# Values of four query tiles in one burst, and W_out landing in the keys' ring, in a two-layer decoder trunk

## The chip, the cores and the metric

The kernel runs on one core of one Trainium2 chip. The metric is the device time of one execution in microseconds (us); each kernel is run several times and the median stands. A profile is one execution with the hardware profiler on. The engines are called as the profile does: PE is TensorE (matmuls; PEld its weight loads), DVE is VectorE, ACT is ScalarE, POOL is GpSimd, SP is SyncE, which here issues all DMAs from one queue in order.

## The reference

Two layers over a sequence of 1024 tokens of width 1024, each with a main branch and a memory branch, both gated, and a LayerNorm on the residual. Layer 0's main branch is a causal pooling. Layer 1's is an attention with a forget gate over 16 heads of 64, whose keys and values come from one projection of the stream:

```python
for block of 128 queries:
    logits = q @ k.T * 64 ** -0.5 + (cum[t] - cum[s])      # causal, cum: running sum of log forget gates
    p = softmax(where(mask, logits, -inf))
    out = p @ v
y = concat([out * silu(g_main), y_mem * silu(g_mem)])       # 1536 wide
x = layer_norm(4 ** 0.25 * x + y @ w_out[1])
```

## The kernel before

All float32 products are made of two or three matmuls of a high and a low part (`hi_lo`: ACT copies the high part in fp32r, DVE subtracts it from the source). A weight of 1 MB is a *slab*: it comes in two pieces of 256 KB, each is loaded to a buffer of the ring "raw" (four buffers), split into high and low in the ring "w" (six buffers, so three pieces), and used by 24 matmuls 128x512; a slab has 48 (L180), 24576 columns. While `low[0]` is set, which is the case in the attention of layer 1, POOL does the splits of slabs (L145, L146).

The change lies in the attention of layer 1, function `fox`. It runs over 16 heads, in pairs. A head has eight *steps*; step i makes tile 7 - i of 128 queries, from the widest (1024 keys) to the narrowest. `probs` makes the logits on PE (L168, two halves in the PSUM ring "L" of two banks), adds the forget row R and takes the minimum on DVE (L715), and the exponential on ACT (L723). In the next step `halves` writes them as a high and a low half in float16 (L744 on ACT, L745 on DVE), and `turn` transposes both with one DMA from SP (L754) into a buffer of ring "T" (six buffers). `LAG` is 5: five steps after a tile's logits PE multiplies it with the values (`values`; matmuls 128x128 in float16, called a *burst* here). Before, an even tile starts a burst for itself and the tile above it: tiles 7 and 6 in step 6 of their head, then 5 and 4, 3 and 2, 1 and 0 in steps 0, 2 and 4 of the next. They go to one PSUM buffer O (one bank, 256 columns used), and two instructions on 64 partitions evict them (L770 ACT, L771 DVE).

PE's order is written out by hand (`tc.manual_schedule(engines={PE})`): logits of the step, a part of the fill (`FRAC`: 0.4), the burst if there is one, the rest of the fill (0.6). The *fill* is matrix work that doesn't depend on the tiles: projections of keys, queries and values of the next pair (three slabs), and gates. Pairs 0, 1, 3, 5 and 6 have three slabs, pairs 2, 4 and 7 four; the fourth or, in pair 7, all four are gates (`gate_ahead`, `late_gate`). Every step gets the same share of fill (`SHARE`). After the last head there are five more steps without logits (`hd == HEADS`), filled by `lead`, which is the first third of layer 1's output projection. A scheduler of the framework sets the order on the other engines, from its own idea of the times; only instructions marked as pinned keep their program order.

`OutProj` brings W_out of layer 1 as 24 pieces of 128x512. `fetch` loads a piece to "raw", `split` makes its high and low part in buffers that the attention no longer needs: the n-th pair of pieces goes to the n-th entry of `wtags`. During pair 7 (heads 14 and 15) pieces 0 to 7 are fetched and split, and `early` brings a third of the branch's output y (columns of the memory branch) for the first 256 tokens, by two DMAs to "raw". In the same time `late_gate` reads the outputs of pairs 3, 5 and 6 back (R, ring of two buffers, shared with the forget rows), multiplies them with their gates on POOL (L790) and stores them again.

The ring "B" has ten buffers of 4 KB per partition; a pair's keys and queries take six of them.

Of the kernel before, what the change touches and what calls it, by code (L numbers as in the profile page):

```python
# [18 lines left out]
P = 128  # L19
# [19 lines left out]
SHARE = (1,1,1,1,1,1,1,1)  # L39
# [32 lines left out]
def trunk_kernel(ctx, tc, x, xT, memT, win, wk, wv0, wv, wmk, wmv, wout, poolw, pscale, lng, lnb, bforget, out):  # L72
# [264 lines left out]
    class OutProj:  # L337
# [45 lines left out]
        def early(self, yh, yl):  # L383
# [153 lines left out]
    with tc.tile_pool(name="in1", bufs=1) as in1:  # L537

        def xy(shape=(P, S)):
            return sb(list(shape), "B", 10, F32R, in1)  # L540

# [208 lines left out]
        def turn(hd, i, two):  # L750

            n = 2 * i + 2
            pt[hd, i] = T([P, 2 * ST, P], F16)
            nc.sync.dma_start_transpose(pt[hd, i][:, :n, :], two[:, : n * P])  # L754

        def values(hd, c, o):

            (v, un), b = pairs[hd // 2][2], hd % 2
            acc = ps([P, 2 * P], "O", 1)
            for i in (2 * c, 2 * c + 1):  # L760
                mm3(
                    acc[:, (i % 2) * P : (i % 2) * P + P],
                    [
                        (v[:, b, 2 * j : 2 * j + 2, :].rearrange("p e d -> p (e d)"), pt[hd, i][:, e * (i + 1) + j, :])
                        for j in range(i + 1) for e in range(2)
                    ],
                )
            own, other = slice(64 * b, 64 * b + 64), slice(64 - 64 * b, P - 64 * b)
            oc = o[own, c * 2 * P : (c + 1) * 2 * P]
# [6 lines left out]
        def pair_out(pr, c, o, g):  # L776

            for k in {1: (3, 2, 1), 0: (0,)}.get(c, ()) if g is not None else ():
                cols = slice(k * 2 * P, (k + 1) * 2 * P)
                nc.gpsimd.tensor_tensor(o[:, cols], o[:, cols], g[:, cols], ALU.mult)  # L780
            if c == 0:
                nc.sync.dma_start(y1d[pr // 4, :, pr % 4, :], o)
# [10 lines left out]
        def fox(following, out_proj):  # L793
# [8 lines left out]
            for hd in range(HEADS + 1):  # L802
# [15 lines left out]
                for i in range(ST if hd < HEADS else LAG):  # L818
                    tile_of = ST - 1 - i
                    ahead = sum(SHARE[i:]) + (sum(SHARE) if b == 0 else 0)  # L820
                    part = fill.left * SHARE[i] / (ahead if hd < HEADS else sum(SHARE[i:LAG]))
# [35 lines left out]
                    if older and older[1] % 2 == 0:  # L857
                        values(older[0], older[1] // 2, older[2])
                        if older[0] % 2:
                            pair_out(older[0] // 2, older[1] // 2, older[2], gs.get(older[0] // 2))  # L860
# [5 lines left out]
        wtags = [("MK", 4), ("V", 4)] + [("B", 10)] * 4 + [("w", 0), ("MK", 4), ("R", 2), ("V", 4), ("PG", 0), ("B", 10)]  # L866
# [69 lines left out]
```

## Time and profile before

| what | value |
|---|---|
| median of 3 runs | 1277.64 us (1276.83 to 1278.07) |
| profiled execution | 1276.2 us, its span 1274.5 us |
| granted clock of PE, mean | 0.992 |
| attention of layer 1 | about 664 to 1146 us of the span |
| PE busy there | 465.4 of 482.0 us |
| DVE, ACT, POOL busy there | 364.1, 324.3, 167.3 us |
| mean busy share of the 16 DMA engines there | 0.76 |

A row of a timeline has the start in us, the length of a merged group, the engine, the line of the kernel, the operation, what it writes and reads, and in brackets the idle time before it with what ended it. Rows of windows give busy time of PE, PEld, DVE, ACT and POOL with the count of instructions, then the granted clock, the share of the DMA engines and GB/s. Matmuls are pipelined: the time per matmul is read from one start to the next.

### The profile page before, as it was taken

To read this page: it belongs to the slowest core of one execution; us is meant where nothing else is said; L and a number is where in the kernel's file an instruction comes from. 1 tells how busy PE (TensorE), PEld (TensorE's weight loads), DVE (VectorE), ACT (ScalarE), POOL (GpSimd) and SP (SyncE) were. 2 spreads that over 40 slices of the span, in tenths; PEclk is the share of its full clock that TensorE was granted. 3 is DMA by queue.
4 is the path that set the end of the run, shared out by engine and by line. 5 is a ranking of instruction groups with operands and counts; after the bars stand their busy time and mean duration, and the time that the engine had idled before them with its cause. 6 is when DMAs were issued, how large, how long until landed. Compare 5 with 4: busy or idle time off the path is not lost. (4 is left out here: it accounts for less than half of the span.)

```text
span 1274.5 us, 19683 instructions
## 1 busy us (share of the span) xinstructions
PE 1245.2 (98%) x7018; PEld 1035.8 (81%) x7018; DVE 803.1 (63%) x1901; ACT 578.3 (45%) x1273; POOL 172.5 (14%) x276
## 2 busy tenths in 40 slices
PE   9999999999999999999999999999999998989997
PEld 6888888888888888888887778887888786868885
DVE  6444766366455555376457888777878887654644
ACT  5233643242321123266226677766767776542110
POOL 0000000000000000000013334343333332420000
PEclk9999999999999999999999999999999999989998
DMA  6333543242453323254517686867968697784430
GB/s 228 103 100 100 124 120 121 83 124 86 158 200 106 103 82 126 75 125 107 161 51 189 134 194 154 187 164 181 185 156 179 158 197 169 159 232 172 166 115 34
DMA packets 267427, 178.66 MB, mean 140 GB/s; under 512 B 212288, under 2 KB 225728, under 8 KB 267328
## 3 DMA queue, kind: packets, MB, share of 16 engines
q1 hardware_dynamic: 267328, 177.40, 52.6%
q8 instruction: 55, 0.90, 0.3%
q14 instruction: 44, 0.36, 0.1%
HBM read 94.97 MB, written 22.61 MB: 92 GB/s over the span
## 5 line engine op out<-in xcount | busy, mean ns | idle before, releaser
L180 PE MATMUL pj<-A,w 128*128 128x512 f32 x2928 | 725.3, 395 | 10.8 <-POOL w L145 9.2
L180 PEld LDWEIGHTS pj<-A,w 128*128 128x128 f32 x2928 | 537.2, 189 | 114.9 <-POOL w L145 9.6
L142 DVE TENSOR_TENSOR w<-raw,w 128x512 fp32r<-128x512 f32 x106 | 73.6, 695 | 105.5 <-ACT w L141 104.6
L723 ACT ACTIVATE T<-MK,s 128x512 f32<-128x512 f32 x192 | 110.8, 577 | 51.6 <-DVE s L715 39.2
L141 ACT CAST w<-raw 128x512 fp32r<-128x512 f32 x106 | 65.7, 621 | 149.0 <-PE pj L180 102.8
L745 DVE SCALAR_TENSOR_TENSOR P<-T,s,P 128x512 f16<-128x512 f32 x192 | 111.8, 614 | 31.6 <-ACT P L744 29.7
L744 ACT ACTIVATE P<-T,s 128x512 f16<-128x512 f32 x192 | 102.7, 576 | 46.4 <-ACT T L723 17.6
L168 PE MATMUL L<-B,B 128*128 128x512 f32 (+3 forms) x384 | 91.3, 343 | 5.0 <-DVE s L715 4.7
L168 PEld LDWEIGHTS L<-B,B 128*128 128x128 f32 x384 | 70.3, 188 | 25.9 <-DVE s L715 12.7
L620 POOL MEMSET G<- 128x128 f32 x1 | 0.2, 204 | 609.5 <-DVE V L334 609.5
L168 PEld LDWEIGHTS <-V 128*128 128x128 f16 x1152 | 66.8, 100 | 19.4 <-issue 18.9
L715 DVE CUSTOM_DVE_ANT_0 MK<-L,R 128x512 f32<-128x512 f32 (+3 forms) x128 | 72.9, 570 | 11.7 <-PE L L168 8.2
L168 PE MATMUL O<-T,V 128*128 128x128 f16 x1152 | 77.7, 223 | 1.7 <-DVE G L771 1.7
L142 DVE TENSOR_TENSOR T<-T,T 128x1024 fp32r<-128x1024 f32 x23 | 28.1, 1222 | 68.2 <-PE L L377 50.4
L146 POOL TENSOR_TENSOR w<-raw,w 128x512 fp32r<-128x512 f32 x54 | 69.7, 1291 | 3.8
L141 ACT CAST T<-T 128x1024 fp32r<-128x1024 f32 x23 | 24.2, 1052 | 99.0 <-DMA T<-y0d 50.5
L707 POOL TENSOR_SCALAR_AFFINE_SELECT R<-R 128x128 f32<-128x128 f32 x128 | 41.1, 327 | 172.3 <-DVE s L715 150.0
L145 POOL TENSOR_SCALAR w<-raw 128x512 fp32r<-128x512 f32 x54 | 35.4, 656 | 143.4 <-PE pj L180 130.4
L213 PE MATMUL pj<-T,w 128*128 128x256 f32 x384 | 48.7, 284 | 0.9 <-DVE w L142 0.8
L213 PEld LDWEIGHTS pj<-T,w 128*128 128x128 f32 x384 | 47.6, 192 | 2.0 <-DVE w L142 1.3
L377 PE MATMUL pj<-B,T 128*128 128x512 f32 x186 | 46.5, 392 | 0.5 <-DVE T L142 0.5
L377 PE MATMUL L<-B,T 128*128 128x512 f32 x174 | 43.0, 391 | 0.0
(214 smaller groups left out, 1598.6 us busy)
## 6 DMA issues: line engine op xcount, KB each, us to landing
raw<-in_win_dram SPq DMA_DIRECT2D x96, 256.0 KB, 2.8
raw<-in_wout_dram SPq DMA_DIRECT2D x48, 256.0 KB, 2.9
B<-B SPq DMA_DIRECT2D x32, 256.0 KB, 3.9
R<-cumd SPq DMA_DIRECT2D x16, 512.0 KB, 4.4
y0d<-Y SPq DMA_DIRECT2D x12, 512.0 KB, 3.1
T<-y0d SPq DMA_DIRECT2D x12, 512.0 KB, 4.1
T<-y1d SPq DMA_DIRECT2D x11, 512.0 KB, 4.0
raw<-in_wmk_dram SPq DMA_DIRECT2D x16, 256.0 KB, 2.6
```

The lines of the kernel that those rows point to most:

```text
L141: pin(nc.scalar.copy(hi, src))
L142: pin(nc.vector.tensor_tensor(lo, src, hi.bitcast(F32), ALU.subtract))
L146: nc.gpsimd.tensor_tensor(lo, src, hi.bitcast(F32), ALU.subtract)
L168: nc.tensor.matmul(acc, a, b, start=i == 0, stop=i == len(terms) - 1)
L180: nc.tensor.matmul(accs[n], a[:, k, :], b[:, kt, n * NH : (n + 1) * NH], start=kt == 0 and i == 0, stop=kt == KT - 1 and i == 2,)
L213: nc.tensor.matmul(acc, w[:, k, :], m[pc][:, k, :], start=pc == 0 and k == 0 and i == 0, stop=pc == 1 and k == 3 and i == 2,)
L377: nc.tensor.matmul(accs[a][nh], y[:, k, a * P : (a + 1) * P], w, start=kt == 8 and i == 0, stop=kt == 7 and i == 2,)
L707: nc.gpsimd.affine_select(R[:, qs], R[:, qs], [[-1, P]], ALU.is_ge, -NEG, base=0, channel_multiplier=1).ins
L715: nc.vector.tensor_tensor_reduce(p[:, lo:up], lg, R[:, lo:up], 1.0, top, ALU.add, ALU.min, m[:, n : n + 1])
L723: nc.scalar.activation(e, p[:, lo:up], AF.Exp, bias=top, scale=-1.0, accum_out=sums[:, n, hd % 2, i : i + 1],)
L744: nc.scalar.activation(pair[:, lo:up], e, AF.Copy, scale=r)
L745: nc.vector.scalar_tensor_tensor(pair[:, L + lo : L + up], e, r, pair[:, lo:up], ALU.mult, ALU.subtract)
```

## The change

- `values` takes four tiles at once: 7 to 4 (52 matmuls) in step 0 of the next head, and 3 to 0 (20 matmuls) in its step 4. O uses its whole bank of 512 columns, and the two evictions take 64x512 each. `pair_out` multiplies with the gate in two parts of two POOL instructions instead of three and one.
- Tiles 2 and 0 are transposed into the second half of the buffer of tiles 3 and 1, so a head takes six buffers of T instead of eight.
- The fill of a step is a share of what is left of fill and values together, less the step's own values: `VALUES` says that step 0 has 52 x 128 columns and step 4 has 20 x 128. It is never below zero.
- In pair 7 the first eight pieces of W_out are loaded by twos into buffers of ring B (`fetch_two`), in steps 0, 1, 5 and 11, and `early` loads its third of y by one DMA into a buffer of B, too. Their splits are placed anew, and the first three entries of `wtags` change places. Pieces 8 to 11 go to "raw" ahead of the five last steps.

```diff
-SHARE = (1,1,1,1,1,1,1,1)
+VALUES = {0: 52 * P, 4: 20 * P}
...
+        def fetch_two(self, land):
+
+            n = self.n + len(self.raws)
+            for j in range(2):
+                nc.sync.dma_start(land[:, j, :], wout[self.l, n // 2 % 2, 2 * self.KKS[n // 4] + j])
+                self.raws.append(land[:, j, :])
...
-            for j in range(2):
-                r, two = raw([P, 2, 2 * P]), slice(2 * j, 2 * j + 2)
-                nc.sync.dma_start(r, self.yd[2, :, two, : 2 * P])
-                yield
-                hi_lo(yh[:, two, :], yl[:, two, :], r, True)
+            nc.sync.dma_start(y, self.yd[2, :, :, : 2 * P])
+            yield
+            for two in (slice(0, 2), slice(2, 4)):
+                hi_lo(yh[:, two, :], yl[:, two, :], y[:, two, :], True)
                 yield
...
+        def land(shape):
+            return sb(list(shape), "B", 10, F32, in1)
...
-            pt[hd, i] = T([P, 2 * ST, P], F16)
-            nc.sync.dma_start_transpose(pt[hd, i][:, :n, :], two[:, : n * P])
+            if i in (2, 0):
+                to = pt[hd, i + 1][:, n + 2 :, :]
+            else:
+                to = T([P, 2 * ST, P], F16)
+            pt[hd, i] = to
+            nc.sync.dma_start_transpose(to[:, :n, :], two[:, : n * P])
...
-            acc = ps([P, 2 * P], "O", 1)
-            for i in (2 * c, 2 * c + 1):
+            acc = ps([P, NH], "O", 1)
+            for i in range(4 * c, 4 * c + 4):
...
-            oc = o[own, c * 2 * P : (c + 1) * 2 * P]
+            oc = o[own, c * NH : (c + 1) * NH]
...
-            for k in {1: (3, 2, 1), 0: (0,)}.get(c, ()) if g is not None else ():
+            for k in (2 * c + 1, 2 * c) if g is not None else ():
...
-                    ahead = sum(SHARE[i:]) + (sum(SHARE) if b == 0 else 0)
-                    part = fill.left * SHARE[i] / (ahead if hd < HEADS else sum(SHARE[i:LAG]))
+                    last = ST + LAG if hd == HEADS else (hd | 1) * ST + ST
+                    at = ST if hd == HEADS else hd * ST
+                    todo = [VALUES.get(k % ST, 0) if k >= ST else 0 for k in range(at + i, last)]
+                    part = max(0, (fill.left + sum(todo)) / len(todo) - todo[0])
...
-                        out_proj.fetch((0, 0, 1, 2, 3, 4, 5, 6, 6, 6, 7, 7, 7, 8, 8, 8)[step])
+                        if step in (0, 1, 5, 11):
+                            out_proj.fetch_two(land((P, 2, NH)))
                         if step == 9:
-                            lead = out_proj.early(*(xy((P, 4, 2 * P)) for _ in range(2)))
-                        if step in (9, 12):
+                            lead = out_proj.early(land((P, 4, 2 * P)), *(xy((P, 4, 2 * P)) for _ in range(2)))
                             next(lead)
+                    if hd == HEADS and i == 0:
+                        out_proj.fetch(12)
...
-                        out_proj.split((0, 0, 0, 1, 2, 3, 4, 5, 6, 6, 6, 6, 7, 7, 8, 8)[step], True)
-                        if step in (11, 15):
+                        out_proj.split((0, 0, 0, 1, 2, 3, 4, 5, 5, 5, 5, 6, 6, 6, 7, 8)[step], True)
+                        if step in (12, 13):
                             next(lead)
...
-                    if older and older[1] % 2 == 0:
-                        values(older[0], older[1] // 2, older[2])
+                    if older and older[1] % 4 == 0:
+                        values(older[0], older[1] // 4, older[2])
...
-        wtags = [("MK", 4), ("V", 4)] + [("B", 10)] * 4 + [("w", 0), ("MK", 4), ("R", 2), ("V", 4), ("PG", 0), ("B", 10)]
+        wtags = [("B", 10), ("V", 4), ("MK", 4)] + [("B", 10)] * 3 + [("w", 0), ("MK", 4), ("R", 2), ("V", 4), ("PG", 0), ("B", 10)]
```

Where the instructions stand is shown at three places. First SP's queue in head 14, before. The tiles named T with a transpose from P are the turned probabilities, raw the ring for loads; raw2303 is the second piece of W_in for late gate 3:

```order
L351 DMA raw2296_11920<-in_wout_dram 128x512
L754 DMA_TRANSPOSE T2284_11864<-P2275_11839 128x10x128
L782 DMA y1d_172<-G2040_10825 128x1024
L150 DMA raw2303_11941<-in_win_dram 128x512
L754 DMA_TRANSPOSE T2295_11911<-P2291_11897 128x8x128
L351 DMA raw2308_11996<-in_wout_dram 128x512
L754 DMA_TRANSPOSE T2306_11952<-P2301_11934 128x6x128
L150 DMA raw2330_12070<-in_win_dram 128x512
```

And now. Here raw2319 and raw2337 are the last two pieces of W_in of the pair (late gate 6); T2156 takes tile 0 of head 13, T2189, T2199 and T2213 take tiles 7, 6 and 5 of head 14:

```order
L150 DMA raw2319_12185<-in_win_dram 128x512
L570 DMA_TRANSPOSE V2161_11457<-MK2157_11445 128x16x64 x2
L767 DMA_TRANSPOSE T2156_11436<-P2171_11482 128x2x128
L767 DMA_TRANSPOSE T2189_11588<-P2186_11574 128x16x128
L150 DMA raw2337_12257<-in_win_dram 128x512
L767 DMA_TRANSPOSE T2199_11632<-P2196_11617 128x14x128
L767 DMA_TRANSPOSE T2213_11685<-P2208_11664 128x12x128
L358 DMA raw2347_12318<-in_wout_dram 128x512
```

The loads of W_in have moved ahead of head 14's transposes, and those of W_out that pass through raw are pieces 8 and later. Second, PE at the end of a burst in head 15's first step, before (O2334 the burst of tiles 5 and 4 of head 14, pj2328 a bank of the fill):

```order
L168 LDWEIGHTS V2215_11595
L168 MATMUL O2334_12083<-T2269_11814,V2215_11595 128x128
L180 MATMUL pj2328_12068<-A500_3025,w2332_12073 128x512
L180 MATMUL pj2328_12068<-A500_3025,w2331_12072 128x512
L180 MATMUL pj2328_12068<-A501_3026,w2331_12072 128x512
```

And now (O2272 the burst of tiles 7 to 4 of head 14, L2278 and L2280 the logits of tile 6 of head 15):

```order
L168 LDWEIGHTS V2161_11457
L168 MATMUL O2272_11927<-T2189_11588,V2161_11457 128x128
L168 MATMUL L2278_11991<-B2014_10810,B2061_11010 128x512
L168 MATMUL L2278_11991<-B2016_10812,B2061_11010 128x512
L168 MATMUL L2280_11998<-B2014_10810,B2061_11010 128x384
L168 MATMUL L2280_11998<-B2016_10812,B2061_11010 128x384
L180 MATMUL pj2267_11917<-A501_3026,w2270_11921 128x512
```

Fill followed the burst before; now the logits of the next tile do. Third, POOL around the first late gate, before (R2277 is the late gate's output, w and raw the splits of W_in, AFFINE_SELECT the mask on the forget row of head 15):

```order
L146 TENSOR_TENSOR w2305_11944<-raw2303_11941,w2304_11943 128x512
L145 TENSOR_SCALAR w2331_12072<-raw2330_12070 128x512
L146 TENSOR_TENSOR w2332_12073<-raw2330_12070,w2331_12072 128x512
L790 TENSOR_TENSOR R2277_11848<-R2277_11848,G2278_11849 128x256 x2
L145 TENSOR_SCALAR w2357_12187<-raw2356_12185 128x512
L790 TENSOR_TENSOR R2277_11848<-R2277_11848,G2278_11849 128x256 x2
L707 AFFINE_SELECT R2243_11710<-R2243_11710 128x128
L146 TENSOR_TENSOR w2358_12188<-raw2356_12185,w2357_12187 128x512
```

And now (R2222 the late gate's output, R2190 the forget row of head 15):

```order
L716 AFFINE_SELECT R2190_11599<-R2190_11599 128x128
L145 TENSOR_SCALAR w2320_12187<-raw2319_12185 128x512
L146 TENSOR_TENSOR w2321_12188<-raw2319_12185,w2320_12187 128x512
L803 TENSOR_TENSOR R2222_11748<-R2222_11748,G2223_11749 128x256 x4
L716 AFFINE_SELECT R2190_11599<-R2190_11599 128x128 x3
L145 TENSOR_SCALAR w2338_12259<-raw2337_12257 128x512
L146 TENSOR_TENSOR w2339_12260<-raw2337_12257,w2338_12259 128x512
L716 AFFINE_SELECT R2190_11599<-R2190_11599 128x128
```

The four multiplications of the late gate stand together now, ahead of three masks of head 15 and of the last split.

More of the change, by code (lines that the diff above doesn't have):

```diff
@@ L381, in products, with early @@
                             yield NH
-        def early(self, yh, yl):
-            for j in range(2):
-                r, two = raw([P, 2, 2 * P]), slice(2 * j, 2 * j + 2)
-                nc.sync.dma_start(r, self.yd[2, :, two, : 2 * P])
-                yield
-                hi_lo(yh[:, two, :], yl[:, two, :], r, True)
+        def early(self, y, yh, yl):
+            nc.sync.dma_start(y, self.yd[2, :, :, : 2 * P])
+            yield
+            for two in (slice(0, 2), slice(2, 4)):
+                hi_lo(yh[:, two, :], yl[:, two, :], y[:, two, :], True)
                 yield
@@ L752, in turn @@
             n = 2 * i + 2
-            pt[hd, i] = T([P, 2 * ST, P], F16)
-            nc.sync.dma_start_transpose(pt[hd, i][:, :n, :], two[:, : n * P])
+            if i in (2, 0):
[4 more added lines that the diff above has]
+            nc.sync.dma_start_transpose(to[:, :n, :], two[:, : n * P])
         def values(hd, c, o):
             (v, un), b = pairs[hd // 2][2], hd % 2
-            acc = ps([P, 2 * P], "O", 1)
-            for i in (2 * c, 2 * c + 1):
+            acc = ps([P, NH], "O", 1)
+            for i in range(4 * c, 4 * c + 4):
                 mm3(
-                    acc[:, (i % 2) * P : (i % 2) * P + P],
+                    acc[:, (i % 4) * P : (i % 4) * P + P],
                     [
@@ L856, in fox @@
                     older = past[0]
-                    if older and older[1] % 2 == 0:
-                        values(older[0], older[1] // 2, older[2])
+                    if older and older[1] % 4 == 0:
+                        values(older[0], older[1] // 4, older[2])
                         if older[0] % 2:
-                            pair_out(older[0] // 2, older[1] // 2, older[2], gs.get(older[0] // 2))
+                            pair_out(older[0] // 2, older[1] // 4, older[2], gs.get(older[0] // 2))
                     fill.pump(part * (1 - FRAC[0]))
```

## Prediction

> **What bounds the kernel now.** I read the page first: its first rows and the row of granted clock in section 2.
>
> ```profile
> span 1274.5 us, 19683 instructions
> PE 1245.2 (98%) x7018; PEld 1035.8 (81%) x7018; DVE 803.1 (63%) x1901; ACT 578.3 (45%) x1273; POOL 172.5 (14%) x276
> ...
> PEclk9999999999999999999999999999999999989998
> ```
>
> TensorE (PE) is the bound: 98% busy, and no other engine is near. So only three things can save time: PE's idle time, a slow clock, and pitch lost between matmuls. The clock row dips in slice 36 of 40 (1115 to 1147 us), and in the last, where the work ends. Then the waits of PE over the whole span:
>
> ```profile
> engine line waited for: us in total, times, longest us
> PE pj L180 <- POOL w L145: 9.2, 2, 5.5
> PE L L168 <- DVE s L715: 4.7, 11, 0.7
> PE O L168 <- DVE G L771: 1.7, 1, 1.7
> ```
>
> Two waits hold 9.2 us: a fill matmul (L180) that waits for GpSimd (POOL) to split a piece of W_in. The timeline of PE, and then of SP and POOL, around them:
>
> ```profile
> 1076.22 0.40 PE L168 MATMUL L<-B,B 128*128 128x256 f32 x2
> 1082.15 3.00 PE L180 MATMUL pj<-A,w 128*128 128x512 f32 x5 [5.54 <-POOL w L145]
> ...
> 1115.15 0.40 PE L168 MATMUL L<-B,B 128*128 128x256 f32 x2
> 1119.15 3.00 PE L180 MATMUL pj<-A,w 128*128 128x512 f32 x5 [3.61 <-POOL w L145]
> ```
>
> ```profile
> 1076.84 0.53 SPq L782 DMA_DIRECT2D y1d<-G  x1
> 1077.46 0.38 SPq L150 DMA_DIRECT2D raw<-in_win_dram  x1
> ...
> 1081.48 0.62 POOL L145 TENSOR_SCALAR w<-raw 128x512 fp32r<-128x512 f32 x1 [3.08 <-DMA raw<-in_win_dram]
> ...
> 1113.84 0.53 SPq L791 DMA_DIRECT2D y1d<-R  x1
> 1114.46 0.39 SPq L150 DMA_DIRECT2D raw<-in_win_dram  x1
> ...
> 1118.36 0.74 POOL L145 TENSOR_SCALAR w<-raw 128x512 fp32r<-128x512 f32 x1 [3.94 <-DMA raw<-in_win_dram]
> ```
>
> Both are the same event, in step 6 of head 14 and in step 6 of head 15 (the two matmuls 128x256 are tile 1). The piece of W_in was issued 4.0 us (1077.46 to 1081.48) and 3.9 us (1114.46 to 1118.36) before POOL could start on it, and PE ran dry meanwhile. The DMA was not slow; it was issued late. The order shows why: its buffer in the ring "raw" was held by W_out pieces, and it stood in SP's queue behind a store. What these stalls did to the clock, by windows:
>
> ```profile
> 1076.62:1082.15 5.53, 0.00 (x0) 0.00 (x0) 4.40 (x14) 3.74 (x9) 1.82 (x4) 0.82 1.05 262
> 1082.15:1087.00 4.85, 4.71 (x25) 3.39 (x25) 0.00 (x0) 0.00 (x0) 2.46 (x3) 0.50 0.74 190
> ...
> 1119.15:1124.60 5.45, 5.32 (x30) 3.98 (x31) 0.00 (x0) 0.00 (x0) 1.51 (x2) 0.50 0.98 209
> 1124.60:1130.00 5.40, 5.40 (x32) 4.53 (x30) 3.57 (x7) 3.77 (x9) 2.36 (x3) 1.00 0.64 170
> ...
> 1126.00:1146.60 20.60, 18.37 (x112) 14.66 (x111) 14.63 (x23) 12.10 (x23) 6.99 (x7) 1.00 0.75 229
> ```
>
> After each stall PE works for 4.85 and 5.45 us at a granted clock of 0.50, then at 1.00.
>
> **W_out in the keys' ring.** Pieces 0 to 7 of W_out no longer pass through "raw". In SP's new order the last two pieces of W_in for pair 7 stand ahead of the transposes of head 14's tiles 7 and 6, where before they stood in the middle of heads 14 and 15. They are needed ten steps later, so both stalls go: 9.15 us (5.54 + 3.61). The slow clock goes with them: half of 4.85 + 5.45 us, 5.15 us. What is late next? SP waits in turn for POOL to free a "raw" buffer, and so holds up a transpose by a step or so; POOL multiplies late gate 3 (four instructions, L803) before it masks R for tiles 6 to 4 of head 15. I put both into the new waits below. The pieces and their splits on ScalarE (ACT) and VectorE (DVE) stay the same in number; the early third of y comes in one DMA instead of two, and W_out in as many as before.
>
> [...]
>
> **One burst of four tiles.** The matmuls are the same ones, 1152 of values and all fills. What falls away is the change between the two kinds: 64 bursts become 32. Its price is read from a head with nothing in the way:
>
> ```profile
> 1021.96 1.85 PE L168 MATMUL O<-T,V 128*128 128x128 f16 x30
> 1023.61 1.41 PE L180 MATMUL pj<-A,w 128*128 128x512 f32 x5
> 1024.86 0.34 PE L168 MATMUL L<-B,B 128*128 128x128 f32 x2
> ...
> 1028.69 1.09 PE L180 MATMUL pj<-A,w 128*128 128x512 f32 x4
> 1029.62 1.40 PE L168 MATMUL O<-T,V 128*128 128x128 f16 x22
> 1030.83 1.41 PE L180 MATMUL pj<-A,w 128*128 128x512 f32 x5
> 1032.08 0.98 PE L168 MATMUL L<-B,B 128*128 128x512 f32 x4
> 1032.89 2.24 PE L180 MATMUL pj<-A,w 128*128 128x512 f32 x9
> 1034.97 0.85 PE L168 MATMUL L<-B,B 128*128 128x512 f32 x4
> ```
>
> From start to start, 30 values take 1.65 us and 22 take 1.21: 0.055 each and nothing left over. The nine fills without a burst take 2.08 us, 0.231 each; the five behind a burst take 1.25, against 1.155 at that rate. So a burst costs 0.095 us beyond its matmuls, and 32 fewer save 3.0 us. If a long burst cost twice as much the saving would be 0; if a boundary with the first fill was undercounted, 4. I keep 3.0.
>
> The evictions halve in number and double in width:
>
> ```profile
> L770 ACT ACTIVATE G<-O,unscale x64: 457/468/475, 693.8 to 1145.8; 64x256 f32<-64x256 f32 x64
> L771 DVE SCALAR_TENSOR_TENSOR G<-O,unscale,G x64: 457/484/492, 694.5 to 1146.6; 64x256 f32<-64x256 f32 x64
> ...
> L657 ACT ACTIVATE B<-pj x32: 581/592/595, 656.7 to 1041.0; 64x512 fp32r<-64x512 f32 x32
> ...
> L658 DVE SCALAR_TENSOR_TENSOR B<-pj,B x32: 683/688/695, 657.8 to 1042.1; 64x512 fp32r<-64x512 f32 x32
> ```
>
> Two 64x256 on DVE cost 0.97 us, one 64x512 (as L658) 0.69; ACT 0.94 against 0.59. Over 32 that frees 9.0 us of DVE and 11.0 of ACT. PE does not wait for that as such, so by itself I cost it at nothing: PE's 98% hides it. The bank is read out 1.28 us (0.59 + 0.69) after a burst, and the next burst is four steps away, so the wait of 1.7 us for it (at the end of head 15, where two bursts stood two steps apart) should go: 1.7.
>
> **Fills by steps.** Of each head, step 0 now holds 52 values and step 4 holds 20, and the fill is what levels the columns: in a pair with three slabs (73728 + 18432) / 16 = 5760 columns a step, less than 52 x 128 = 6656, so step 0 has no fill and the others about 11 matmuls instead of 9. The 4.7 us of waits of L168 for DVE fell on steps without a burst, where PE had 9 x 0.231 = 2.1 us between two logits; now it has 2.5. I take 2.9 of the 4.7 as gone (0 and 4.7 are the bounds).
>
> **The new waits.** A burst now starts directly behind the logits of tile 7, and needs tile 4's transpose. In the tightest head the transpose stood so (SP), with the landings of all 128 of them:
>
> ```profile
> 1024.60 1.79 SPq L754 DMA_TRANSPOSE T<-P  x1
> ...
> DMA to landing us min/median/max: 2.3/3.7/7.6
> ```
>
> Issued at 1024.60, used at 1029.62: 5.0 us. The 0.93 us of fill ahead of that burst (1028.69 to 1029.62) is gone, and 4.1 us stay, against a median of 3.7 and a maximum of 7.6. Nine of the sixteen bursts of tiles 7 to 4 fall in such short steps (in pairs with three slabs). Zero is one end; the other is 1 us in each of nine, 9. Most heads will fit as the median does; I take 2.5 for these, for POOL's new order and for SP's waits.
>
> **The sum.** - 9.15 - 5.15 - 3.0 - 1.7 - 2.9 + 2.5 = -19.4. The profiled execution took 1276.2 us (its span 1274.5), which becomes 1256.8. The median of the runs, 1277.64, is 1.4 above the profiled one, so I expect 1258.2, and say 1258.
>
> **Rivals.**
> (a) Transposes late. The bursts wait for tile 4 in the nine heads: 9 instead of 2.5, 1265. For it: a 0.4 us margin at the median. Against: not one burst of before waited for a transpose.
> (b) The stalls stay, or pair 7 gets a new one: SP in its order, blocked by POOL, holds the weights after all, and only the other terms come: 1277.6 - 3.0 - 1.7 - 2.9 + 2.5 = 1272.5. For it: L803 x4 stands ahead of masks and of the last split. Against: that split is needed only six steps on.
> [...]
> (d) More gain: all three waits go (4.7 + 1.7 + 9.15), with 5.15 of slow clock and 4 for the changes of kind, and nothing new comes: 1277.6 - 24.7 = 1253.
>
> **Chances.** My forecast with (d) as its lower end 0.78, (a) 0.10, (b) 0.06, (c) 0.04, a mixture near no change 0.02. The range runs from 1252 (just below (d)) to 1267 (past (a)) and leaves (b), (c) and some misses out. A difference of 0.2% (2.6 us) is about what a measurement can tell from none: faster 0.92, same 0.03, slower 0.05.
>
> **What would show it.** After: no row "PE pj L180 <- POOL w L145" of more than 1 us; clock 1.00 throughout heads 14 and 15; 32 groups of L168 O with 52 or 20 rows, 0.055 us apart also at the end of the 52; the waits of L168 for DVE below 2.5 us. I am wrong if bursts show waits "<-DMA T<-P", if SP's wait for POOL leaves POOL's split waiting for a DMA again, or if values late in a long burst come slower than 0.055.

## The result, and the profile after

| kernel | median of the runs | profiled execution | its span | mean granted clock |
|---|---|---|---|---|
| before | 1277.24 us (1275.49 to 1278.07) | 1276.2 us | 1274.5 us | 0.992 |
| after | 1255.49 us (1254.45 to 1256.91) | 1256.91 us | 1255.2 us | 0.996 |

The ratio is 0.9825, with a 95% interval of 0.9807 to 0.9843: faster by 1.6 to 1.9%. The forecast was 1258 us (1252 to 1267). The profiled execution of after is the slowest of its four; against the profiled one of before it is 19.3 us shorter, and the sum in the prediction said 19.4. The terms of that sum do not all agree so well.

The first rows of the page of after, and its row of granted clock:

```profile
PE 1238.4 (99%) x7018; PEld 1039.0 (83%) x7018; DVE 797.2 (64%) x1869; ACT 570.4 (45%) x1241; POOL 170.7 (14%) x276
...
PEclk9999999999999999999999999999999999999999
```

The number of matmuls is the same, 7018, and PE is busy for 6.8 us less: part of this is clock, part is pitch. The 32 instructions that DVE and ACT have lost are the evictions. What PE waits for in after:

```profile
PE L L168 <- DVE s L724: 4.8, 8, 1.1
...
PE O L168 <- DMA T<-P: 0.2, 1, 0.2
```

The 9.2 us for POOL are gone, and so are the 1.7 us for the O bank. The 4.7 us for DVE (L715 before, L724 now) are still there. All bursts together waited 0.2 us for a transpose. What is left out here lies outside the attention. Stretches of heads 14 and 15 (us, then busy time of PE, PEld, DVE, ACT and POOL, granted clock, share of the DMA engines, GB/s):

```profile
1076.60:1126.00 49.40, 48.42 (x324) 40.35 (x323) 38.88 (x90) 31.96 (x70) 18.46 (x27) 1.00 0.94 224
1126.00:1146.60 20.60, 20.60 (x92) 17.04 (x92) 8.09 (x9) 6.50 (x9) 2.39 (x2) 1.00 0.74 262
```

Clock 1.00, and 0.98 us of idle time in 49.40 us, where the two stalls and their slow windows stood.

To size the rest, the attention is cut out from its first logits to the first matmul of the output projection that follows it. The rows are before, after, and after once more in a later job (the run `e8_after_again` below):

```profile
672.06:1144.94 472.88, 456.69 (x2881) 373.09 (x2880) 361.49 (x1029) 322.14 (x750) 165.36 (x263) 0.99 0.77 176
```

```profile
673.00:1126.51 453.51, 448.24 (x2881) 374.83 (x2880) 355.96 (x997) 313.98 (x717) 162.43 (x262) 1.00 0.82 184
```

```profile
671.88:1124.91 453.03, 446.55 (x2881) 373.74 (x2880) 355.87 (x997) 313.91 (x717) 162.47 (x262) 1.00 0.82 184
```

The stage took 472.88 and takes 453.51, 19.4 us less (the work ahead of it took 0.9 us longer in that execution, what follows 0.8 less). PE's idle time there fell from 16.2 us (472.88 - 456.69) to 5.3: 10.9. Of its busy time 10.05 us before and 3.41 in after were at a granted clock of 0.50, none in the repetition; half of that is counted as lost, an estimate from the granted clock: 5.0 us and 1.7. Without that, the same 2881 matmuls took 451.7 us and now take 446.5 (456.69 - 5.02, 448.24 - 1.71): 5.1 less. So the 19.4 are 10.9 of idle time, 3.3 of clock and 5.1 of matmul time proper, to the rounding. This last column of "busy at full clock" is used throughout below.

### The profile page after: what moved, and what is told of

It is laid out like the page before. It is cut to its first block, busy times and chain, and to the rows that moved or that the text cites. A ratio compares the mean times of both kernels' runs of the same rounds, so it can differ in the third digit from the quotient of the medians.

```text
span 1255.2 us, 19617 instructions
## 1 busy us (share of the span) xinstructions
PE 1238.4 (99%) x7018; PEld 1039.0 (83%) x7018; DVE 797.2 (64%) x1869; ACT 570.4 (45%) x1241; POOL 170.7 (14%) x276
## 5 line engine op out<-in xcount | busy, mean ns | idle before, releaser
L180 PE MATMUL pj<-A,w 128*128 128x512 f32 x2928 | 711.7, 394 | 0.3 <-ACT A L141 0.3
L168 PE MATMUL L<-B,B 128*128 128x512 f32 (+3 forms) x384 | 92.4, 345 | 5.0 <-DVE s L724 4.8
L168 PEld LDWEIGHTS L<-B,B 128*128 128x128 f32 x384 | 69.5, 188 | 23.2 <-DVE s L724 11.3
L724 DVE CUSTOM_DVE_ANT_0 MK<-L,R 128x512 f32<-128x512 f32 (+3 forms) x128 | 72.8, 569 | 13.5 <-PE L L168 8.3
L168 PEld LDWEIGHTS <-V 128*128 128x128 f16 x1152 | 64.4, 98 | 8.8 <-issue 8.1
L168 PE MATMUL O<-T,V 128*128 128x128 f16 x1152 | 69.9, 219 | 0.2 <-DMA T<-P 0.2
```

Of the source, the lines that this page charges most:

```text
L168: nc.tensor.matmul(acc, a, b, start=i == 0, stop=i == len(terms) - 1)
L180: nc.tensor.matmul(accs[n], a[:, k, :], b[:, kt, n * NH : (n + 1) * NH], start=kt == 0 and i == 0, stop=kt == KT - 1 and i == 2,)
L724: nc.vector.tensor_tensor_reduce(p[:, lo:up], lg, R[:, lo:up], 1.0, top, ALU.add, ALU.min, m[:, n : n + 1])
```

## The experiments

The kernel before ran beside every job: 1277.28, 1278.94 and 1277.99 us in the three. All times are medians.

| run | time, us (lowest to highest) | ratio to before, 95% | attention, us | PE idle there | of it logits for DVE | lost to the clock | busy at full clock |
|---|---|---|---|---|---|---|---|
| e1_landing_alone | 1262.96 (1261.38 to 1265.47) | 0.9886 (0.9867 to 0.9905) | 460.9 | 9.6 | 6.0 | 0 | 451.3 |
| e2_burst_alone | 1267.62 (1267.27 to 1268.10) | 0.9921 (0.9907 to 0.9935) | 462.0 | 13.1 | 4.4 | 1.7 | 447.2 |
| e3_equal_fill | 1257.13 (1255.98 to 1258.65) | 0.9841 (0.9825 to 0.9857) | 453.5 | 6.4 | 6.3 | 0 | 447.1 |
| e4_bursts_of_two | 1259.75 (1257.89 to 1261.19) | 0.9858 (0.9840 to 0.9876) | 456.2 | 6.1 | 3.3 | 0 | 450.0 |
| e5_fill_inside | 1260.64 (1260.25 to 1260.89) | 0.9859 (0.9839 to 0.9880) | 456.9 | 7.2 | 6.8 | 0 | 449.7 |
| e6_two_evictions | 1254.60 (1253.36 to 1257.32) | 0.9816 (0.9796 to 0.9836) | 450.9 | 4.1 | 3.7 | 0 | 446.8 |
| e7_fill_in_step0 | 1256.86 (1256.62 to 1259.44) | 0.9830 (0.9813 to 0.9847) | 456.3 | 6.5 | 6.1 | 1.7 | 448.1 |
| e8_after_again | 1254.74 (1254.72 to 1255.34) | 0.9815 (0.9798 to 0.9832) | 453.0 | 6.5 | 6.1 | 0 | 446.6 |
| e9_evict_later | 1255.00 (1254.76 to 1255.98) | 0.9823 (0.9810 to 0.9836) | 451.3 | 4.8 | 4.5 | 0 | 446.5 |
| e10_minimum_first | 1252.67 (1251.32 to 1254.26) | 0.9803 (0.9789 to 0.9817) | 449.6 | 4.3 | 4.1 | 0 | 445.3 |

The last five columns are of the profiled execution. Of e2, 4.0 us of the idle time lie at the very end of the stage. The waits of the logits (L168) for DVE, that is for a minimum of the tile before, are 4.8 us in after and 6.1 in e8, the same program: a difference of 1.3 us between two executions says nothing here.

**The two halves of the change, each alone.** The first is the kernel before with only W_out's new landing (`fetch_two`, `land`, `early`, the splits' places, `wtags`):

```diff
-                        out_proj.fetch((0, 0, 1, 2, 3, 4, 5, 6, 6, 6, 7, 7, 7, 8, 8, 8)[step])
+                        if step in (0, 1, 5, 11):
+                            out_proj.fetch_two(land((P, 2, NH)))
...
-        wtags = [("MK", 4), ("V", 4)] + [("B", 10)] * 4 + [("w", 0), ("MK", 4), ("R", 2), ("V", 4), ("PG", 0), ("B", 10)]
+        wtags = [("B", 10), ("V", 4), ("MK", 4)] + [("B", 10)] * 3 + [("w", 0), ("MK", 4), ("R", 2), ("V", 4), ("PG", 0), ("B", 10)]
```

> The kernel before, with only W_out's first eight pieces and y's third landing in ring B (their splits placed as in the changed kernel, pieces 8 to 11 fetched ahead of the five last steps); bursts of two tiles and equal shares of fill stay. My theory: the two waits of L180 for POOL (9.15 us) and the slow clock after them (5.15 us) both come from W_out in ring raw. They go, and the time is 1277.2 - 14.3 = 1263 us (1261 to 1265), with waits of L168 for DVE still 4 to 5 us. Rival: the stalls go because the new fill by steps asks for the pieces of W_in at other times. Then at least one of them stays here, and the time is 1270 us or more.

It took 1262.96 us, 14.3 less than before. Its waits of PE:

```profile
PE L L168 <- DVE s L724: 6.0, 11, 1.9
PE O L168 <- DVE G L780: 1.7, 1, 1.7
PE O L168 <- DMA T<-P: 1.5, 1, 1.5
```

The time is the theory's; the waits for DVE, which it had at 4 to 5 us, are 6.0. The stalls for POOL are gone with the landing alone, and with them the slow clock. The wait for the O bank, 1.7 us, stays with the bursts of two (e4, which has bursts of two as well, has one of 1.3). Matmul time proper is as before (451.3 against 451.7). The second half is the rest of the change without the landing:

```diff
-                        if step in (0, 1, 5, 11):
-                            out_proj.fetch_two(land((P, 2, NH)))
+                        out_proj.fetch((0, 0, 1, 2, 3, 4, 5, 6, 6, 6, 7, 7, 7, 8, 8, 8)[step])
...
-        wtags = [("B", 10), ("V", 4), ("MK", 4)] + [("B", 10)] * 3 + [("w", 0), ("MK", 4), ("R", 2), ("V", 4), ("PG", 0), ("B", 10)]
+        wtags = [("MK", 4), ("V", 4)] + [("B", 10)] * 4 + [("w", 0), ("MK", 4), ("R", 2), ("V", 4), ("PG", 0), ("B", 10)]
```

> The changed kernel, with W_out's landing put back: pieces through ring raw, one by one, y's third by two DMAs. Bursts of four tiles and the fill by steps stay. My theory: the stalls of L180 for POOL come back, some 9 us with a slow clock of some 5 us behind them, and only bursts, fill and evictions gain: 1277.2 less 4 to 8 us, 1269 to 1273 us. Rival: if the fill by steps had cured the stalls, 1256 to 1260 us, with no wait of L180 over 1 us.

It took 1267.62 us, 9.7 less than before, just under the interval of the theory and far above the rival's. Its waits:

```profile
PE L L168 <- DVE s L715: 4.4, 7, 1.1
PE pj L377 <- ACT T L141: 4.0, 1, 4.0
PE pj L180 <- POOL w L145: 2.8, 1, 2.8
PE pj L180 <- POOL w L146: 1.4, 2, 0.9
```

With the old landing the waits for POOL are back, though smaller (4.2 us instead of 9.2), and a new one of 4.0 us stands where the output projection starts. So the burst does not remove the stalls by itself, though it shortens them, which neither theory had; the landing removes them. Alone the two halves save 14.3 + 9.7 = 24.0 us, together 21.8.

**The price of a change of kind.** The changed kernel with bursts of two again, four to a head, each with its own share in the levelled fill:

```diff
-VALUES = {0: 52 * P, 4: 20 * P}
+VALUES = {6: 30 * P, 0: 22 * P, 2: 14 * P, 4: 6 * P}
...
-            for i in range(4 * c, 4 * c + 4):
+            for i in (2 * c, 2 * c + 1):
...
-                    if older and older[1] % 4 == 0:
-                        values(older[0], older[1] // 4, older[2])
+                    if older and older[1] % 2 == 0:
+                        values(older[0], older[1] // 2, older[2])
```

> The changed kernel with bursts of two tiles (eight transposes to eight buffers of T a head, evictions of 64x256, 64 bursts), its fill levelled by the columns of these bursts (30, 22, 14 and 6 of 128 in steps 6, 0, 2 and 4). W_out lands in ring B. My theory: a change between fill and values costs 0.095 us, so 32 more of them cost 3.0 us, and the levelled steps wait no more for DVE than the changed kernel: 1258 to 1260 us. Rival: the changes of kind cost nothing that a kernel feels, and the time is that of the changed kernel, 1255.5 within 1 us, or less since no step is without fill.

It took 1259.75 us, in the theory's range. The difference to e8 lies in the matmul time proper (450.0 against 446.6) and not in the idle time (6.1 against 6.5). Then the changed kernel with one matmul of fill inside each burst:

```diff
-        def values(hd, c, o):
+        def values(hd, c, o, middle):
...
+                if i == 4 * c + 2:
+                    middle()
...
-                        values(older[0], older[1] // 4, older[2])
+                        values(older[0], older[1] // 4, older[2], lambda: fill.pump(NH))
```

> The changed kernel, with one matmul of fill put inside each burst, behind its second tile: the matmuls are the same ones, and PE changes between the two kinds 32 times more. If a change costs what the prediction read, 0.095 us for a burst, 3.0 us more than the changed kernel: 1258.5 (1257 to 1260). If, as the comparison of the two traces says (451.7 us of matmul time proper in the attention became 446.5), it costs 0.11 to 0.16: 1259 to 1260.6. Rival: the change of kind costs nothing, and the 3 to 5 us came from the levelled fill and from shorter queues: 1255.5 and no more.

It took 1260.64 us, 5.9 more than the changed kernel of the same job (e8), and a little above both ranges. The end of a burst in a head without waits, first in e5, then in after:

```profile
999.83 1.00 PE L168 MATMUL O<-T,V 128*128 128x128 f16 x15
1000.64 0.47 PE L180 MATMUL pj<-A,w 128*128 128x512 f32 x1
1000.96 1.85 PE L168 MATMUL O<-T,V 128*128 128x128 f16 x30
1002.62 1.08 PE L168 MATMUL L<-B,B 128*128 128x512 f32 x4
```

```profile
999.81 2.73 PE L168 MATMUL O<-T,V 128*128 128x128 f16 x46
1002.35 1.39 PE L168 MATMUL L<-B,B 128*128 128x512 f32 x4
```

The single fill takes 0.32 us from its start to the next value (1000.64 to 1000.96), against the 0.231 us of one among many: 0.09 over. Over the stage PE is busy 449.69 us at full clock against 446.55 in e8: 3.1 us for 32 more changes, 0.098 each. Bursts of two (e4) give 450.00 - 446.55 = 3.5, 0.108 each. The prediction's 0.095 us was right; what was too low in the expectation is the rest of the time. The other 2.8 us by which e5 is longer in time lie elsewhere: 0.7 of PE's waits, 0.7 after the stage, 1.0 ahead of it, where the two programs are alike, and the rest between the two executions and their medians.

**The levelled fill.** The changed kernel with the same share of fill in every step:

```diff
-VALUES = {0: 52 * P, 4: 20 * P}
+VALUES = {}
```

> The changed kernel with equal shares of fill in every step (no account of the values' columns). My theory: a burst of 52 beside a full share makes step 0 long and leaves 2.1 us of fill in the others, so L168 waits more for DVE: 3 to 6 us more in PE's waits, time 1257 to 1262 us. Rival: DVE's lag behind the wide tiles in steps 1 and 2 is what is left in the changed kernel (two waits of 1.1 us in 865 and 980 us), and more fill in step 0 gives DVE time there: 1252 to 1255 us.

It took 1257.13 us, at the lower edge of the theory, whose mechanism did not show: the waits for DVE are 6.3 us, against 4.8 and 6.1, and not 3 to 6 us more. The profile has the attention as long as after's (453.5). The levelling is worth 1.6 to 2.4 us by the medians, with intervals that overlap, and none by the profiled executions. And the changed kernel with some fill left in step 0:

```diff
-VALUES = {0: 52 * P, 4: 20 * P}
+VALUES = {0: 36 * P, 4: 20 * P}
```

> The changed kernel, with step 0 counted as 36 x 128 columns of values instead of 52 x 128, so that in pairs with three slabs it keeps 2 to 3 matmuls of fill and the other steps give them up. Theory: the 4.8 us of waits for DVE that are left lie where step 0 has no fill and two logits follow one burst, so the fill gives DVE its time: waits below 2.5 us, no slow clock, 1252.5 to 1254.5. Rival: the waits only move to the later steps, which have less fill then, as with the equal fill: 1255 to 1258.

It took 1256.86 us, 2.1 more than e8. The theory failed and the rival's account held. The waits for DVE did not fall, they spread over more steps: 6.1 us in 13 waits, against 6.1 in 10 in e8. The matmul time proper rose by 1.5 us. In the three-slab pairs step 0 got one matmul of fill on each side of the burst (at 862.31 and 865.44 us in head 7), and of the two the second took 0.31 us, to the logits at 865.75, against 0.231 among many; the first took 0.24, to the burst.

**The evictions.** The changed kernel with two pairs of 64x256 evictions for a burst:

```diff
-            oc = o[own, c * NH : (c + 1) * NH]
-            nc.scalar.activation(oc, acc[other, :], AF.Copy, scale=un[own])
-            nc.vector.scalar_tensor_tensor(oc, acc[own, :], un[own], oc, ALU.mult, ALU.add)
+            for half in range(2):
+                oc, ac = o[own, c * NH + half * 2 * P : c * NH + (half + 1) * 2 * P], acc[:, half * 2 * P : (half + 1) * 2 * P]
+                nc.scalar.activation(oc, ac[other, :], AF.Copy, scale=un[own])
+                nc.vector.scalar_tensor_tensor(oc, ac[own, :], un[own], oc, ALU.mult, ALU.add)
```

> The changed kernel, with each burst evicted by two pairs of 64x256 instructions instead of one pair of 64x512: some 9 us of DVE and 11 us of ACT come back. Theory: PE hides it, as the prediction costed it: 1255.5 to 1256.5. Rival: the eviction stands in DVE's queue ahead of the minimum that PE's logits wait for in step 0, and 0.28 us more of it lengthens eight or more waits and may bring a slow clock: 1257.5 to 1260, with waits of L168 for DVE of 7 us instead of 4.8.

It took 1254.60 us, against 1254.74 for e8: nothing. The evictions in after, by their tile:

```profile
L783 ACT ACTIVATE G<-O,unscale x32: 678/684/690, 701.6 to 1130.0; 64x512 f32<-64x512 f32 x32
L784 DVE SCALAR_TENSOR_TENSOR G<-O,unscale,G x32: 733/750/759, 702.4 to 1130.7; 64x512 f32<-64x512 f32 x32
```

One 64x512 costs 0.750 us on DVE and 0.684 on ACT, so with two 64x256 at 0.97 and 0.94 the one eviction saves 7.0 and 8.2 us of these engines (the prediction had 9.0 and 11.0, from instructions of another tile). None of it reached the time, as costed. The rival's waits of 7 us did not come either: with more for DVE to do (361.0 us in the attention instead of 355.9) the logits waited 3.7 us for it. Why less, the next part shows.

**Where the waits for DVE come from.** PE in after around head 7's first steps, a burst of 52 and the logits on both sides of it:

```profile
856.88 1.24 PE L168 MATMUL L<-B,B 128*128 128x512 f32 x4
857.95 3.08 PE L168 MATMUL O<-T,V 128*128 128x128 f16 x52
860.84 1.07 PE L168 MATMUL L<-B,B 128*128 128x512 f32 x4
861.75 2.70 PE L180 MATMUL pj<-A,w 128*128 128x512 f32 x11
865.54 0.73 PE L168 MATMUL L<-B,B 128*128 128x512 f32 x2 [1.09 <-DVE s L724]
866.74 0.51 PE L168 MATMUL L<-B,B 128*128 128x256 f32 x2 [0.46 <-DVE s L724]
```

and DVE in the same stretch:

```profile
862.21 0.21 DVE L742 TENSOR_SCALAR s<-sums 128x1 f32<-128x1 f32 x1 [1.59 <-ACT T L732]
862.46 0.16 DVE L745 RECIPROCAL s<-s 128x1 f32<-128x1 f32 x1
863.42 0.75 DVE L754 SCALAR_TENSOR_TENSOR P<-T,s,P 128x512 f16<-128x512 f32 x1 [0.80 <-ACT P L753]
864.14 0.74 DVE L784 SCALAR_TENSOR_TENSOR G<-O,unscale,G 64x512 f32<-64x512 f32 x1
864.80 0.67 DVE L724 CUSTOM_DVE_ANT_0 MK<-L,R 128x512 f32<-128x512 f32 x1
```

The logits started at 860.84 are tile 6's. Their minimum (L724) runs only at 864.80, though DVE had stood idle for 1.59 and 0.80 us in between: a sum that waits for ACT, a low half that waits for ACT, and the burst's eviction stand ahead of it in DVE's queue. The next tile needs the same bank, and PE waits. At this place it is an order, not a lack of DVE time. Two runs move these instructions behind the minimum, with no wait added. First the eviction:

```diff
+            def evict():
+                nc.scalar.activation(oc, acc[other, :], AF.Copy, scale=un[own])
+                with tc.issue_after(least[0]):
+                    nc.vector.scalar_tensor_tensor(oc, acc[own, :], un[own], oc, ALU.mult, ALU.add)
+
+            return evict
...
                         fresh[0] = probs(hd, tile_of, R, sums, inverse, behind)
+                        release()
```

Here `least[0]` is the last minimum recorded, and `release` runs the evictions held from the step before, with their gate.

> The changed kernel, with each burst's eviction recorded one step later and held on DVE behind the minimum of the next tile (no wait, only the place in DVE's queue). Theory: the waits of PE's logits for DVE that are left (4.8 and 6.1 us in two profiles) come from DVE's order, in which the eviction of 0.74 us, and the low halves, stand ahead of a minimum that could go sooner. Moving the eviction takes 0.74 us from each of seven or eight waits behind a burst: waits of 2 to 3.5 us, no slow clock, 1252 to 1254. Rival: the minimum is late for another reason (it waits for the exponential's sum, or PE's own logits), and the waits stay between 4.5 and 6.5 us: 1254.5 to 1256.

Then the low halves as well:

```diff
-                nc.vector.scalar_tensor_tensor(pair[:, L + lo : L + up], e, r, pair[:, lo:up], ALU.mult, ALU.subtract)
+                with tc.issue_after(least[0]):
+                    nc.vector.scalar_tensor_tensor(pair[:, L + lo : L + up], e, r, pair[:, lo:up], ALU.mult, ALU.subtract)
```

> The same with the low halves of a tile (P) held on DVE behind the last minimum of the next tile too. Theory: then nothing that waits for ACT stands ahead of a minimum, and the pairs of waits of 1.1 and 0.46 us at the three-slab pairs go altogether: waits below 1.5 us, 1251 to 1253. Rival: the halves now come later, and with them the transposes, so that bursts wait for T and the exponentials for their bank: 1254 to 1258, with waits for DMA T<-P or DVE MK instead.

The times were 1255.00 and 1252.67 us. In e9 the theory failed and the rival's figures came: no gain that can be measured, and 4.5 us of waits. e10 is faster than e9, beside which it ran, with ranges that do not touch; that it is faster than after is not shown (0.9803, 0.9789 to 0.9817, of before, against 0.9825 and 0.9815 with intervals that overlap). Its time is in the theory's range, but not for the theory's reason: the waits for DVE are 4.1 us instead of below 1.5, and of the 1.7 us by which its attention is shorter than e9's, 1.2 are matmul time proper. At the place shown above e10 has:

```profile
862.32 1.07 PE L168 MATMUL L<-B,B 128*128 128x512 f32 x4
863.24 2.69 PE L180 MATMUL pj<-A,w 128*128 128x512 f32 x11
865.77 0.85 PE L168 MATMUL L<-B,B 128*128 128x512 f32 x4
...
869.77 0.51 PE L168 MATMUL L<-B,B 128*128 128x256 f32 x2 [0.29 <-DVE s L724]
```

The logits of the same tile (865.77) no longer wait. In e9, with the eviction alone moved, the first of the two waits of after (1.09 us) had fallen to 0.10 there and the second was as before:

```profile
867.15 0.51 PE L168 MATMUL L<-B,B 128*128 128x256 f32 x2 [0.46 <-DVE s L724]
```

The minimum starts 3.96 us after the first logits of its tile in after (860.84 to 864.80), 2.96 in e9 (862.25 to 865.21) and 0.75 in e10 (862.32 to 863.07). So the order makes the waits behind that burst, first the eviction's place and then the low halves'; 0.29 us stand one tile later. The sum that waits for ACT still stands ahead of the minimum in e10, with 1.33 us of idle DVE time before it, so the edit does less than its expectation says. And e6, with two evictions, shows the same from the other side:

```profile
864.63 0.73 PE L168 MATMUL L<-B,B 128*128 128x512 f32 x2 [0.26 <-DVE s L724]
865.62 0.50 PE L168 MATMUL L<-B,B 128*128 128x256 f32 x2 [0.26 <-DVE s L724]
```

There only the first half of the eviction stands ahead of the first minimum (863.90) and the second half comes behind it (864.55). DVE is also 0.5 us earlier there: tile 7's minimum starts 0.53 us after the burst (857.88 to 858.41) instead of 1.05. So DVE has more to do, and the waits at this place are 1.0 us less. In e7 0.48 us are left there.

In the whole attention the totals differ too little (4.8 and 6.1 for one program) to rank after, e6, e9 and e10 by them. Most of what is left in e10 are waits of 0.6 to 1.0 us in later steps of heads 1, 3 and 13. In head 13, DVE and then PE:

```profile
1030.86 0.69 DVE L667 SCALAR_TENSOR_TENSOR B<-pj,B 64x512 fp32r<-64x512 f32 x1
...
1031.78 0.48 DVE L724 CUSTOM_DVE_ANT_0 MK<-L,R,s 128x256 f32<-128x256 f32 x1
```

```profile
1032.33 0.50 PE L168 MATMUL L<-B,B 128*128 128x256 f32 x2 [0.94 <-DVE s L724]
```

Between the two minima of a tile (1030.01 and 1031.78) stands an eviction of the fill (L667), with another just ahead (1029.29), and DVE is hardly idle from 1029.29 to 1032.67. Head 3 is alike; in head 1 the second wait has low halves ahead of the minimum as well. Here it is DVE's time as much as its order, and no run moved these. Of e10's gain in matmul time proper one thing can be seen: the four logits of tile 5 in head 7, which a wait cuts in two in after, take 1.08 us there beside that wait (865.54 to 867.08, less 0.46) and 0.68 in e10 (865.77 to 866.45). So the column "busy at full clock" holds 0.40 us at that tile that came with the wait. The rest of the gain is not explained.

**The changed kernel again.**

> The changed kernel once more, on the same chip as the others of this call: 1255.5 (1254.4 to 1257). If the 1.7 us at a clock of 0.50 behind two short waits come and go between executions, its granted clock is 0.996 in some runs and 0.998 in others, with the time 1.5 us longer at 0.996; were they fixed by the program, all runs would show the same clock.

It took 1254.74 us, with clock 0.998 in all four runs; in after's own four runs the clock was 0.996 twice (1255.99 and 1256.91 us) and 0.998 twice (1254.45 and 1255.00). The slow stretch comes and goes between executions of the same program; what the traces show of it is in the last section.

## Why the prediction was right, and where a step failed

The total was right, 1258 against 1255.5, and the working was right where most of the time lay. Term by term, from the profiled executions:

| term | predicted, us | measured, us | by |
|---|---|---|---|
| stalls for POOL | -9.15 | -9.2 | waits before and after; gone in e1, 4.2 back in e2 |
| slow clock | -5.15 | -3.3, and -5.0 in the repetition | windows |
| changes of kind | -3.0 | -3.1 to -3.5, of 5.1 less matmul time proper | e5, e4 |
| wait for the O bank | -1.7 | -1.7 | waits; stays in e1 |
| waits for DVE | -2.9 | +0.1, and +1.4 in the repetition | waits, e7, e9, e10 |
| new waits | +2.5 | +0.2 | waits |

That the sum meets the profiled difference within 0.1 us (19.4 and 19.3) is luck: 3.0 us less came of the waits for DVE and 1.9 less of the clock than it said, and 2.3 us of new waits that did not come and 2.1 more of matmul time made up for most of it. The stalls, the clock after them and the O bank were read from the two timelines, and each stands as it was said. e1 and e2 divide the change as the sum did: the landing takes the stalls and the clock, the bursts most of the rest. That e1's median is 14.3 us below before, and 9.15 + 5.15 = 14.3, is luck in the last digits: by its ratio it is 12 to 17 us, and in its profiled execution the attention is 12.0 us shorter, since 1.3 us more of waits for DVE and 1.5 for a transpose came with it.

The step "I take 2.9 of the 4.7 as gone" failed. It looked at one gap, from tile 6's logits to tile 5's, where PE has 2.5 us of fill instead of 2.1, and took the wait for a matter of that time. But what step 1 gained, step 0 lost. Head 7 before:

```profile
861.20 1.07 PE L168 MATMUL L<-B,B 128*128 128x512 f32 x4
...
865.47 0.97 PE L168 MATMUL L<-B,B 128*128 128x512 f32 x4
...
868.54 0.73 PE L168 MATMUL L<-B,B 128*128 128x512 f32 x2
```

From tile 7's first logits to tile 5's PE had 7.34 us (861.20 to 868.54), and in e10, where nothing waits there, it has 7.24 (858.53 to 865.77). And DVE's queue fixed when the minimum ran. Before, the eviction ran at 866.42 while DVE stood waiting for ACT, and tile 6's minimum started 2.33 us after its first logits (865.47 to 867.80); in after the eviction comes behind the low half, and it is 3.96. So the waits at this place grew from 0.47 to 1.55 us. A change of DVE's order took them away there (e9 and e10); in the whole attention no run shows the 2.9 us.

The term of the new waits was too large. It counts each wait at its own length, with no slow clock behind it; that was the author's estimate, and after has a slow stretch of 3.41 us behind waits of 1.09 and 0.46 (the last section). The bursts of tiles 7 to 4 do follow the logits at once, but only one of them waited for its transpose, 0.2 us. Rivals (a) and (b) did not come, nor did a kernel slower than before, and of (d) the waits for DVE did not go; its 4 us for the changes of kind lie between the 3.1 to 3.5 that e5 and e4 give them and the 5.1 of the whole matmul time proper.

The price of a change of kind, 0.095 us, was confirmed (0.098 in e5). The whole fall of the matmul time proper was 5.1 us. The sum has nothing for the 1.6 to 2.0 us beyond the bursts. Without the levelling 0.5 of it goes (e3), and with two lone matmuls of fill in step 0 1.5 goes (e7); where the rest comes from is open.

"What would show it" held for the stalls and the bursts, and failed for the waits for DVE (4.8 instead of below 2.5). The clock was 1.00 throughout heads 14 and 15, but not elsewhere, which the prediction had not looked for: in after it was 0.50 for 3.41 us in head 7.

## What to carry to other kernels

The two stalls of the bounding engine were worth their length, 9.2 us, and the slow clock behind them, 5.0, and went when their loads moved forward in the queue (e1). When the engine that is waited for shows idle time just before the late instruction, look at what stands ahead of it in its queue: more work for the waiting engine left such waits at 6.1 us in e7, a change of order took one of 1.09 us away at its place in e10. Where that engine was not idle, as in head 13 of e10 (a wait of 0.94 us), no run shows that an order helps. Time that one step gained by moving fill, another lost here (7.34 us for the two together before, 7.24 in e10): add up the steps. The change from one kind of matmul to another was priced from the starts in a stretch without waits, at 0.095 us, and the price held when 32 of them were put back (0.098).

## What was not expected of the hardware

The prediction counts a new wait at its own length (its upper bound is 1 us in each of nine). In after, waits of 1.09 and 0.46 us close together were followed by a slow stretch. Two stretches of 3.41 us in after:

```profile
863.83:867.24 3.41, 1.85 (x8) 0.99 (x7) 3.41 (x9) 1.96 (x4) 0.29 (x1) 1.00 0.65 152
867.24:870.65 3.41, 3.41 (x10) 2.66 (x9) 3.20 (x10) 2.84 (x8) 0.29 (x1) 0.50 1.08 259
```

PE was idle for 1.56 of 3.41 us, and then had 10 matmuls in the next 3.41 us at clock 0.50. In e8, the same program, the same waits (1.11 and 0.47) stand at 865.60 and 866.80 us with 1.58 us idle in 3.41, and the clock stayed at 1.00. So it did in after itself behind the same two waits at 980 us. In e7 a wait of 1.64 us and one of 0.20 were followed by 3.41 us at 0.50, with 1.84 us idle in the 3.41 ahead of the drop (674.86 to 678.27).

In the attention of every profiled run that has any, the slow stretches are 3.41 us or twice that. Where one execution has several, up to the kernel's end, their starts lie close to a whole number of such stretches apart: 867.24 and 1249.53 us in after (112), 1080.20, 1117.75 and 1267.93 in before (11 and 44), 678.27 and 1251.71 in e7 (168), 1078.43, 1133.04 and 1262.75 in e2 (16 and 38). Each of these differences, divided by its number, gives 3.413 us (after: 382.29 / 112) or 3.414. So the starts fit a grid of such stretches, which lies differently in each execution: the last slow start is at 1249.53 us in after and at 1247.74 in e8. The grid is an estimate from these starts. In e8, 112 stretches ahead of its slow start at 1247.74 us, a line of it (865.45) cuts the two waits into 0.96 and 0.62 us of idle time:

```profile
862.04:865.45 3.41, 2.45 (x11) 1.68 (x9) 2.34 (x5) 2.73 (x6) 0.00 (x0) 1.00 0.69 123
865.45:868.87 3.42, 2.80 (x12) 2.08 (x13) 3.32 (x12) 2.01 (x5) 0.49 (x2) 1.00 0.72 152
```

The waits of after at 980 us are cut alike, into 0.75 and 0.80 (at 979.88, 33 stretches behind 867.24). By this estimate that would be why the same waits are dear in one place and not in the other.

The idle time in a stretch of the grid does not decide it alone. In the attention, drops followed stretches with 1.56 us idle (after), 1.83 and 2.04 (e2), 1.84 (e7), 2.21 and 3.41 (before), and none followed a stretch at clock 1.00 with less (1.53 us in before, 1141.64 to 1145.05, of the wait of 1.7 for the O bank, left it at 1.00). But none followed 1.76 us in e1 (673.34 to 676.75, by its slow start at 1257.02) either, nor 1.9 us in e2 (1071.60 to 1075.02, PE busy 1.52). What else decides is open; no run was made for it. In before, too, a drop came with less than a whole stretch idle ahead of it. Its second stall began at 1115.54 us, and the clock fell 2.2 us into it:

```profile
1114.34:1117.75 3.41, 1.20 (x7) 0.84 (x5) 2.88 (x10) 2.88 (x8) 0.08 (x1) 1.00 1.08 320
1117.75:1121.16 3.41, 1.88 (x4) 1.06 (x5) 1.15 (x3) 0.62 (x2) 2.25 (x3) 0.50 1.24 239
```

So in after two waits with 1.56 us of idle time in 3.41 were followed by 3.41 us at 0.50. With half of that counted as lost, as above, they cost some 1.7 us more than their own length there, an estimate; at 980 us, where the clock stayed at 1.00, they cost none of it.
